# First group in six PSUM banks ordered by kind, early split of two mixed tiles, and another last statistic, in a one-layer streaming encoder

## The chip, the cores and the metric

One Trainium2 chip, one core. The metric is the device time of one launch in microseconds (us), the median of three runs. TensorE is PE (its weight loads PEld), VectorE DVE, ScalarE ACT, GpSimd POOL, and SyncE (SP) issues nearly all DMAs. PSUM has eight banks of 128 x 512 floats; the kernel gives six to products (`psm`) and two to small ones (`pst`).

## The reference, cut to what matters

2048 prompt positions and 8 x 16 sample positions (17 tiles of 128) go through one layer of three parallel mixers, then an output projection and a layer norm:

```python
h = jnp.einsum('btd,de->bte', x, w_in)                    # 1024 -> 2816
a, g_a, u, v, g_b, c1, c2, g_c = jnp.split(h, SPLITS, axis=-1)
y_a = pool_mixer(pool_ext, a, pos0, pool_w, pool_scale)   # trailing means 2/4/8/16, 64x64 products
v_n = layer_norm(v, gmlp_ln_g, gmlp_ln_b)
y_b = u * spatial_mix(v_n, gmlp_w, gmlp_b)                # lower-triangular 128x128 per head
c = c1 * jax.nn.sigmoid(c2)
y_c = conformer_tail(conv_ext, conv_w, ...)               # causal depthwise conv 31, LN, silu, 384x384
mixed = jnp.concatenate([silu(g_a) * y_a, silu(g_b) * y_b, silu(g_c) * y_c], axis=-1)
out = jnp.einsum('bte,ed->btd', mixed, w_out) + b_out     # 1024 -> 1024
x_new = layer_norm(ALPHA * x + out, ln_g, ln_b)
```

All values are float32. A large product is made of three: each operand is split into a rounded high part (`xhi`, `whi`, 32-bit values for the PE) and the rest (`xlo`, `wlo`), and high x high, high x low and low x high are added in PSUM.

## The kernel before

**Blocks and groups.** The 17 tiles are cut into blocks of 6, 6 and 5. For each block, eight groups of weight columns are multiplied one after another (`GROUPS`): group 0 is c2/0, c1/0, c2/1; group 1 is c1/1, c2/2, c1/2; then ga and a, v, gb, u, and group 7 is gc. x stands in eight rows k of 128 inputs (`XRow`; `xhi0` holds k=0 and 1, and so on), a group's weights in four pieces of two k each (`Piece`). `mm3` walks k from 0 to 7 and, at each k, over its outputs, with three matmuls for each: 12 matmuls a k where four outputs (banks) are open. In every block group 0 opens four banks for c2/0 and c1/0 (two halves of up to 384 columns each) and then walks all k again for c2/1.

**Splitting.** A load lands in one of four staging buffers (`stage`). ACT casts it to the high part, DVE subtracts to get the low part (`split`; the low part is recorded 1 us later by the planner's clock), and the subtraction frees the buffer for the next load. `Loader` keeps the four buffers full and splits a job when its `next` is called: by `hook(plan)` after the k of a group that the plan names, or by `after(us, fn)`. High and low weight parts go round in rings of six (`RING`). In block 0 each group's parts are also written to DRAM (`put`, tiles `keep`), and blocks 1 and 2 load them from there without splitting (`Kept`).

**Order.** Nothing is moved by a scheduler at run time: engines take their instructions in the order of the recording. `Clock.pe` counts planned PE time, `after` puts a function on a heap, and `poll` records what is due after each k. The 31 convolution taps of each channel tile (`conv`: `acc`, DVE, over all positions of the block) fill DVE whenever its planned clock is behind PE's; what is left at a block's end is recorded at once (`drain`), before the sums over channels (`csum`), whose low part `slo` the PE needs for `ps_mean`.

**Ends.** Mixed outputs go to DRAM tiles `mix`. During group 7 of block 2, `Mixed` loads whole tiles back (two staging buffers each) and `WPart` loads w_out in twelve parts (three for each pair of k, in the buffers of x that PE has left). The output projection opens four banks for tiles 0 and 1 together; two of them are banks that hold gc until ACT has taken its Silu (`sgc`). Then tiles 2 to 16 follow one by one. The last tile ends with its statistics (`lmv`), 1/sqrt(var + eps) as `inverse` on POOL (a multiply-add and a power), two passes on DVE in halves, and a store of each half.

The lines of the start that the change touches are these:

```python
    rows.append(XRow(0, k, lambda k=k: nc.sync.dma_start(out=w0[:, k, :], in_=wv[:, k, :])))
```

x rows 0 and 1 are loaded in two pieces each (384 columns), with one k of the first weights between the two pieces, and are split by halves.

Of the kernel before, what the change touches and what calls it, by code (L numbers as in the profile page):

```python
# [14 lines left out]
D = 1024  # L15
P = 128
# [57 lines left out]
def encoder_kernel(ctx: ExitStack, tc: tile.TileContext, a):  # L74
# [61 lines left out]

    warm = const.tile([P, 1], F32, name="warm")
    nc.vector.memset(warm, 0.0)
    nc.scalar.activation(out=warm, in_=warm, func=AF.Silu)
    mhalf = const.tile([P, 1], F32, name="mhalf")  # L140
    nc.gpsimd.memset(mhalf, -0.5)
    onec = const.tile([P, 1], F32, name="onec")
# [23 lines left out]
    class Piece:  # L166
# [7 lines left out]
        def split(self, then=None):  # L174
            hi = core.tile([P, 2, 384], F32R, tag="whi", bufs=RING, name="whi")
            lo = core.tile([P, 2, 384], F32R, tag="wlo", bufs=RING, name="wlo")
            split(hi[:, :self.n, :self.cols], lo[:, :self.n, :self.cols], self.st, then)
            ring.setdefault(self.key, []).append((hi, lo))
            if self.keep is not None:
                after(3, lambda: put(self.keep, hi, lo, self.cols))  # L180

    def put(keep, hi, lo, cols):
        for x, part in enumerate((hi, lo)):
# [15 lines left out]
        hi, lo = ring[key][k // 2]  # L199
        return hi[:, k % 2, c0:c0 + n], lo[:, k % 2, c0:c0 + n]  # L200

    def mm3(outs, kdim=KT, hook=None):

        for k in range(kdim):
            for ps, lhs, rhs in outs:
                lh, ll = lhs(k)
                rh, rl = rhs(k)
                nc.tensor.matmul(ps, lh, rh, start=(k == 0), stop=False)  # L208
                nc.tensor.matmul(ps, lh, rl, start=False, stop=False)  # L209
                nc.tensor.matmul(ps, ll, rh, start=False, stop=(k == kdim - 1))  # L210
# [11 lines left out]
    def w_in(key, g):  # L222

        w = len(GROUPS[g]) * P
        v = a["w_in"][:, gofs[g]:gofs[g] + KT * w].rearrange("p (k c) -> p k c", k=KT)
        if key[0] == 0:
            kept[g] = [dram.tile([P, 2, 2, w], F32, name=f"keep{g}_{k0}") for k0 in range(0, KT, 2)]
        keep = kept[g] if key[0] == 0 else [None] * (KT // 2)
        return [lambda k0=k0: Piece(key, v[:, k0:k0 + 2, :], w, keep[k0 // 2]) for k0 in range(0, KT, 2)]

    kept = {}
# [4 lines left out]
        w = len(GROUPS[g]) * P  # L236
        return [lambda k=k: Kept((b, g), k, kept[g][k], w, g % 2 == 1 and k < 2) for k in range(KT // 2)]

    def put_first():
        hi, lo = ring[0, 0][0]  # L240
        put(kept[0][0], hi, lo, 384)

    xhi = [None] * (KT // 2)
    xlo = [None] * (KT // 2)
# [40 lines left out]
    ring[0, 0] = [(whi0, wlo0)]  # L285
    rows = []
    for k in range(2):
        rows.append(XRow(0, k, lambda k=k: nc.sync.dma_start(out=w0[:, k, :], in_=wv[:, k, :])))
    w1 = wg[1]()
    for k in range(2):  # L290
        nc.vector.tensor_copy(whi0[:, k, :], w0[:, k, :])
        nc.vector.tensor_tensor(out=wlo0[:, k, :], in0=w0[:, k, :], in1=whi0[:, k, :].bitcast(F32),
                                op=ALU.subtract)
        rows[k].split(halves=True)
    w1.split()
    for k in range(2, KT, 2):
        rows = [XRow(0, k), XRow(0, k + 1)]
# [62 lines left out]
        nc.gpsimd.affine_select(out=w, in_=w, compare_op=ALU.is_ge, fill=0.0, base=0,  # L360
                                pattern=[[0, 4], [1, P]], channel_multiplier=-1)

    after(5, put_first)
    after(12, load_pool)
    after(24, load_v)
    after(130, load_small)
# [90 lines left out]
    def c_in(b, todo, wkey, hook=None):  # L457

        T, Tp = len(BLOCKS[b]) * P, prompt_width(b)
        runs, pss = [], {}  # L460
        for what, j, c0 in todo:
            if what == "c2":
                drain(j)
                ext = cp.tile([P, CONVC + TMAX], F32, tag=f"cext{j}", name=f"cext{j}")
                conv_state[(b, "ext", j)] = ext
                nc.gpsimd.tensor_copy(ext[:, 0:CONVC], halo_c[:, j, :])
            for t0, n in splits(T):
                ps = psm.tile([P, 512], F32, tag="mm", name="ps_c")
                pss[(what, j, t0)] = ps
                runs.append((ps[:, :n], lambda k, c0=c0: wslice(wkey, k, c0, P),  # L470
                             lambda k, t0=t0, n=n: xslice(k, t0, n)))
        if len(todo) > 1:
            mm3(runs)
        for what, j, c0 in todo:
            ext = conv_state[(b, "ext", j)]
            for t0, n in splits(T):
                if len(todo) == 1:
                    mm3([runs.pop(0)], hook=hook if t0 > 0 else None)
                ps = pss[(what, j, t0)]
                m = max(min(n, Tp - t0), 0)  # L480
                pieces = []
                if m > 0:
                    pieces.append((ext[:, CONVC + t0:CONVC + t0 + m], ps[:, :m]))
                if m < n:
                    pieces.append((exts[:, j, :, CONVC:], ps[:, m:n].rearrange("p (b t) -> p b t", b=NB)))
                for e, p in pieces:
                    if what == "c2":
                        nc.scalar.activation(out=e, in_=p, func=AF.Tanh, scale=0.5)
                    else:
                        vec.scalar_tensor_tensor(out=e, in0=e, scalar=1.0, in1=p,  # L490
                                                       op0=ALU.add, op1=ALU.mult)
            if what == "c1":
# [380 lines left out]
    def group_work(b, g, hook):  # L873
# [3 lines left out]
            {"v": b_v, "gb": b_gate, "u": b_u}[what](b, key, hook)  # L877
        elif what in ("c1", "c2"):
            todo = [(w, j, c * P) for c, (w, j) in enumerate(group)]
            if g == 0:  # L880
                c_in(b, todo[:2], key)
                todo = todo[2:]
            for i, t in enumerate(todo):
# [10 lines left out]
    for b in range(len(BLOCKS)):  # L894
# [4 lines left out]
        for g in range(LASTG):  # L899
            if b == 0 or (b, g + 1) == (LASTB, LASTG):  # L900
                loads = Loader([(fn, 1) for fn in w_in((b, g + 1), g + 1)])
                after(6, loads.next)
                after(9, loads.next)
                group_work(b, g, loads.hook({1: 1, 3: 1}))
            else:

                for i, fn in enumerate(w_kept(b, g + 1)):
                    after(10 + i if g % 2 == 0 and i < 2 else 5 + i, fn)
                group_work(b, g, None)
        if b == 0:  # L910
            W = w_kept(b + 1, 0)
            after(5, W[0])
            after(6, W[1])
            loads = Loader([(lambda k=k: XRow(b + 1, k), 1) for k in range(KT)])

            def leave(k):
                if k in (2, 4):
                    W[1 + k // 2]()
                if 2 <= k < 7:
                    loads.next()  # L920
# [54 lines left out]
    class WPart:  # L975
# [10 lines left out]
        def split(self, then=None):  # L986
# [9 lines left out]
                wo[kp] += [hi, lo]  # L996
            split(hi, lo, self.st[:, :n], then)

    jobs = [(lambda kp=kp, part=part: WPart(kp, part), 1) for kp in range(KT // 2) for part in range(3)]

    jobs[:0] = [(lambda q=q: Mixed(q), 2) for q in range(2)]
    jobs.insert(8, (lambda: Mixed(2), 2))
    loads = Loader(jobs)
    group_work(LASTB, LASTG, loads.hook({1: 2, 2: 1, 3: 2, 4: 1, 5: 2, 6: 1}))
    while loads.out:
        loads.next()
        flush()
# [35 lines left out]
    def out_finish(q, runs, together):  # L1043
# [19 lines left out]
        else:  # L1063

            mv = const.tile([P, 2], F32, name="lmv")
            vec.bn_aggr(out=mv, in_=last.rearrange("p a b -> p (a b)"))
            rs = inverse(mv, "l")
            halves = (slice(0, 512), slice(512, D))
            for c in halves:
                vec.scalar_tensor_tensor(out=y[:, c], in0=y[:, c], scalar=mv[:, 0:1], in1=bc["ln_g"][:, c],  # L1070
                                         op0=ALU.subtract, op1=ALU.mult)
# [107 lines left out]
```

## Time and profile before

| | |
|---|---|
| median of three runs | 776.77 us (776.49 to 778.35) |
| profiled execution | 778.33 us, span 776.6 us |
| PE busy | 765.1 us (99%), 4289 matmuls |
| DVE busy | 619.6 us (80%) |
| ACT busy | 195.5 us (25%) |
| POOL busy | 144.6 us (19%) |
| DMA | 132.91 MB, mean 171 GB/s |

Rows of a timeline read: start, duration (both us), engine, line, operation, out<-in, shape, count, and in brackets the idle time before it and what ended it. A matmul's duration overlaps the next one's; the step from start to start is what it costs. In rows of windows, (x...) counts instructions, and the last three numbers are granted PE clock, DMA share and GB/s. A row of waits reads: engine and instruction, what it waited for, total us, times, longest. A row of DMA issues ends with KB each and the median us from issue to landing. A row of a chain is start, length, engine, tile, line.

### The profile page before, as it was taken

The page shows a single profiled execution, that of the slowest core. Times are in us where ns is not written, and L with a number is a line of the kernel's source. Part 1 is how long each engine was busy: PE and PEld are TensorE (multiplying, and loading weights), DVE is VectorE, ACT ScalarE, POOL GpSimd, SP SyncE. Part 2 cuts the span into 40 slices and gives each one's busy share as a digit, 9 for nine tenths or more (in the row PEclk, how much of TensorE's full clock was granted, in tenths as well). Part 3 has the DMA queues.
Part 4 walks back from the last instruction along what each step waited for, and adds up shares of the span by engine and source line. Part 5 has one row for each costly group of instructions (what it writes and reads, how often), then busy time and mean ns, then how long its engine had stood idle before and what let it go on. Part 6 is the DMA issues. An engine that isn't in the chain of part 4 may idle for free.

```text
span 776.6 us, 11274 instructions
## 1 busy us (share of the span) xinstructions
PE 765.1 (99%) x4289; PEld 727.5 (94%) x4289; DVE 619.6 (80%) x916; ACT 195.5 (25%) x362; POOL 144.6 (19%) x172
## 2 busy tenths in 40 slices
PE   8999999999999999999999999999999999999996
PEld 6999999999999999999999999999988888888885
DVE  5799999999489989898147888899776987666665
ACT  5322314302412130220043122031261233232110
POOL 1010112300001011130002300151006244323241
PEclk9999999999999999999999999999999999999998
DMA  7975866359631465405655147363476434435411
GB/s 247 340 227 183 282 217 244 126 170 309 271 109 42 94 219 209 163 21 175 223 182 191 52 93 215 149 207 114 121 249 264 163 103 142 162 126 169 134 71 68
DMA packets 82118, 132.91 MB, mean 171 GB/s; under 512 B 25104, under 2 KB 48656, under 8 KB 82064
## 3 DMA queue, kind: packets, MB, share of 16 engines
q1 hardware_dynamic: 82064, 132.19, 51.5%
q8 instruction: 33, 0.54, 0.3%
q14 instruction: 21, 0.17, 0.1%
HBM read 90.52 MB, written 41.64 MB: 170 GB/s over the span
## 4 chain that ended last, share of the span: by engine, by line
PE 93%; DMA 3%; DVE 1%; SPq 1%; ACT 1%; issue 0%; POOLq 0%; DVEq 0%; POOL 0%; ACTq 0%
PE ps_o L208 8%; PE ps_o L209 8%; PE ps_o L210 8%; PE ps_c L208 6%; PE ps_c L209 6%; PE ps_c L210 6%; PE ps_gb L208 3%; PE ps_gb L209 3%; PE ps_gb L210 3%; PE ps_v L208 3%; PE ps_v L209 3%; PE ps_v L210 3%; PE ps_u L210 3%; PE ps_u L208 3%; PE ps_u L209 3%; PE ps_gc L210 2%
## 5 line engine op out<-in xcount | busy, mean ns | idle before, releaser
L131 DVE SCALAR_TENSOR_TENSOR acc<-cext,cw,acc 128x768 f32<-128x768 f32 (+1 forms) x270 | 257.7, 954 | 4.1
L208 PE MATMUL ps_o<-woxhi,mhi 128*128 128x512 f32 (+1 forms) x208 | 80.9, 389 | 1.2 <-ACT sgc L547 1.2
L209 PE MATMUL ps_o<-woxlo,mhi 128*128 128x512 f32 (+1 forms) x208 | 80.9, 389 | 0.0
L210 PE MATMUL ps_o<-woxhi,mlo 128*128 128x512 f32 (+1 forms) x208 | 80.3, 386 | 0.0
L208 PE MATMUL ps_c<-xhi,whi 128*128 128x384 f32 (+1 forms) x240 | 79.7, 332 | 0.4 <-ACT xhi L152 0.3
L209 PE MATMUL ps_c<-xlo,whi 128*128 128x384 f32 (+1 forms) x240 | 79.1, 330 | 0.8 <-DVE xlo L131 0.8
L210 PE MATMUL ps_c<-xhi,wlo 128*128 128x384 f32 (+1 forms) x240 | 78.6, 328 | 0.0
L208 PEld LDWEIGHTS ps_o<-woxhi,mhi 128*128 128x128 f32 x208 | 39.1, 188 | 9.8 <-ACT sgc L547 1.6
L209 PEld LDWEIGHTS ps_c<-xlo,whi 128*128 128x128 f32 x240 | 45.2, 188 | 2.2 <-DVE xlo L131 2.2
L208 PEld LDWEIGHTS ps_c<-xhi,whi 128*128 128x128 f32 x240 | 45.4, 189 | 1.5 <-ACT xhi L152 1.2
L210 PEld LDWEIGHTS ps_o<-woxhi,mlo 128*128 128x128 f32 x208 | 39.1, 188 | 8.2
L152 ACT CAST whi<-stage 128x768 fp32r<-128x768 f32 (+1 forms) x39 | 29.9, 770 | 66.2 <-PE ps_u L210 30.9
L131 DVE TENSOR_TENSOR xlo<-stage,xhi 128x768 fp32r<-128x768 f32 (+2 forms) x26 | 21.7, 853 | 31.0 <-ACT xhi L152 30.9
L209 PEld LDWEIGHTS ps_o<-woxlo,mhi 128*128 128x128 f32 x208 | 39.1, 188 | 7.5
L209 PE MATMUL ps_v<-wlo,xhi 128*128 128x384 f32 x136 | 45.5, 334 | 0.0
L208 PE MATMUL ps_v<-whi,xhi 128*128 128x384 f32 x136 | 45.5, 334 | 0.0
L210 PE MATMUL ps_v<-whi,xlo 128*128 128x384 f32 x136 | 45.5, 334 | 0.0
L208 PE MATMUL ps_u<-whi,xhi 128*128 128x384 f32 x136 | 45.4, 334 | 0.0
L209 PE MATMUL ps_u<-wlo,xhi 128*128 128x384 f32 x136 | 45.4, 334 | 0.0
L210 PE MATMUL ps_u<-whi,xlo 128*128 128x384 f32 x136 | 45.4, 334 | 0.0
L210 PEld LDWEIGHTS ps_c<-xhi,wlo 128*128 128x128 f32 x240 | 45.3, 189 | 0.0
L131 DVE TENSOR_TENSOR xr<-xr,ln_g 128x1024 f32<-128x1024 f32 x16 | 29.3, 1832 | 19.8 <-ACT xr L438 19.8
(210 smaller groups left out, 1916.9 us busy)
## 6 DMA issues: line engine op xcount, KB each, us to landing
whi<-keep SPq DMA_DIRECT2D x34, 384.0 KB, 6.0
wlo<-keep SPq DMA_DIRECT2D x34, 384.0 KB, 6.6
stage<-in_w_in SPq DMA_DIRECT2D x27, 384.0 KB, 4.7
keep<-whi SPq DMA_DIRECT2D x24, 384.0 KB, 4.3
keep<-wlo SPq DMA_DIRECT2D x24, 384.0 KB, 4.5
xr<-in_x_prompt SPq DMA_DIRECT2D x16, 512.0 KB, 5.0
o_y<-xr SPq DMA_DIRECT2D x16, 512.0 KB, 2.9
stage<-keep SPq DMA_DIRECT2D x20, 384.0 KB, 7.3
```

The lines of the kernel that those rows point to most:

```text
L131: return fn(*args, **kw)
L152: nc.scalar.copy(hi, src)
L208: nc.tensor.matmul(ps, lh, rh, start=(k == 0), stop=False)
L209: nc.tensor.matmul(ps, lh, rl, start=False, stop=False)
L210: nc.tensor.matmul(ps, ll, rh, start=False, stop=(k == kdim - 1))
```

## The change

1. In block 0, group 0 opens all six banks at once (c2/0, c1/0, c2/1). `mm3` has a parameter `early`: for k below 4 the matmuls of one k are ordered by kind (first half high x high for all outputs, then w high x x low, second half high x high, and so on) and not by output.
2. The first weights are loaded by ACT's queue, and the warm-up Silu stands behind these two issues. DVE makes their low part after the first half's low part of x.
3. Group 0 is no longer kept in block 0. In block 1 it is loaded from `w_in` and split again, through the staging buffers and mixed with the rows of x, and kept then (20 us after the split) for block 2. Group 0's loader splits group 1's pieces at k=3 and 5, not 1 and 3.
4. In the last group of block 2 the two first mixed tiles are split 4 and 5.5 us after its start by the planner's clock; the third comes last, behind all parts of w_out, and the plan of the hook is another.
5. For the last tile ACT makes var + eps (an Identity with a bias), POOL only the power; the parts are 640 and 384 columns.

```diff
-    nc.scalar.activation(out=warm, in_=warm, func=AF.Silu)
...
-                after(3, lambda: put(self.keep, hi, lo, self.cols))
+                after(3 if self.key[0] == 0 else 20, lambda: put(self.keep, hi, lo, self.cols))
...
-    def mm3(outs, kdim=KT, hook=None):
+    def mm3(outs, kdim=KT, hook=None, early=0):
         for k in range(kdim):
-            for ps, lhs, rhs in outs:
+            for half, kind in ((0, 0), (0, 1), (1, 0), (0, 2), (1, 1), (1, 2)) if k < early else ():
+                for ps, lhs, rhs in outs[half::2]:
+                    nc.tensor.matmul(ps, lhs(k)[kind == 2], rhs(k)[kind == 1],
+                                     start=(k == 0 and kind == 0), stop=False)
+            for ps, lhs, rhs in outs if k >= early else ():
...
-        if key[0] == 0:
+        keeps = key[0] == (1 if g == 0 else 0)
+        if keeps:
...
-        rows.append(XRow(0, k, lambda k=k: nc.sync.dma_start(out=w0[:, k, :], in_=wv[:, k, :])))
+        rows.append(XRow(0, k, lambda k=k: nc.scalar.dma_start(out=w0[:, k, :], in_=wv[:, k, :])))
+    nc.scalar.activation(out=warm, in_=warm, func=AF.Silu)
...
+    def first_low(k):
+        nc.vector.tensor_tensor(out=wlo0[:, k, :], in0=w0[:, k, :], in1=whi0[:, k, :].bitcast(F32),
+                                op=ALU.subtract)
     for k in range(2):
         nc.vector.tensor_copy(whi0[:, k, :], w0[:, k, :])
-        nc.vector.tensor_tensor(out=wlo0[:, k, :], in0=w0[:, k, :], in1=whi0[:, k, :].bitcast(F32),
-                                op=ALU.subtract)
-        rows[k].split(halves=True)
+        lows = [lambda k=k: first_low(k)]
+        rows[k].split(lambda: lows.pop()() if lows else None, halves=True)
...
-    after(5, put_first)
...
-            mm3(runs)
+            mm3(runs, hook=hook, early=4 if b == 0 else 0)
...
-            if g == 0:
+            if g == 0 and b == 0:
+                c_in(b, todo, key, hook)
+                todo = []
+            elif g == 0:
...
-                group_work(b, g, loads.hook({1: 1, 3: 1}))
+                group_work(b, g, loads.hook({1: 1, 3: 1} if (b, g) != (0, 0) else {3: 1, 5: 1}))
...
-            W = w_kept(b + 1, 0)
-            after(5, W[0])
-            after(6, W[1])
-            loads = Loader([(lambda k=k: XRow(b + 1, k), 1) for k in range(KT)])
...
-            group_work(b, LASTG, leave)
+            W = [(fn, 1) for fn in w_in((b + 1, 0), 0)]
+            X = [(lambda k=k: XRow(b + 1, k), 1) for k in range(KT)]
+            loads = Loader(W[:2] + X[:1] + W[2:3] + X[1:3] + W[3:] + X[3:])
+            group_work(b, LASTG, loads.hook({1: 1, 2: 1, 3: 2, 4: 2, 5: 2, 6: 2}))
             loads.next(3)
...
-    jobs[:0] = [(lambda q=q: Mixed(q), 2) for q in range(2)]
-    jobs.insert(8, (lambda: Mixed(2), 2))
-    loads = Loader(jobs)
-    group_work(LASTB, LASTG, loads.hook({1: 2, 2: 1, 3: 2, 4: 1, 5: 2, 6: 1}))
+    mix = [(lambda q=q: Mixed(q), 2) for q in range(3)]
+    loads = Loader(mix[:2] + jobs + mix[2:])
+    after(4, loads.next)
+    after(5.5, loads.next)
+    group_work(LASTB, LASTG, loads.hook({1: 1, 2: 2, 3: 1, 4: 2, 5: 1, 6: 2}))
...
-            rs = inverse(mv, "l")
-            halves = (slice(0, 512), slice(512, D))
+            rs = const.tile([P, 1], F32, tag="rs", bufs=4, name="lrs")
+            nc.scalar.activation(out=rs, in_=mv[:, 1:2], func=AF.Identity, scale=1.0, bias=eps)
+            nc.gpsimd.tensor_tensor(out=rs, in0=rs, in1=mhalf, op=ALU.pow)
+            halves = (slice(0, 640), slice(640, D))
```

Three places show what moves. A row is line, operation, out<-in with buffer numbers, and shape.

**PE, the first twelve products.** `ps_c_232` and `_233` are the two halves of c2/0 before (`_228` and `_229` after), `_234`, `_235` those of c1/0 (`_230`, `_231`); after, `_234` and `_235` are c2/1. Before:

```order
L208 MATMUL ps_c_232<-xhi0_110,whi_96 128x384
L209 MATMUL ps_c_232<-xlo0_111,whi_96 128x384
L210 MATMUL ps_c_232<-xhi0_110,wlo_97 128x384
L208 MATMUL ps_c_233<-xhi0_110,whi_96 128x384
L209 MATMUL ps_c_233<-xlo0_111,whi_96 128x384
L210 MATMUL ps_c_233<-xhi0_110,wlo_97 128x384
L208 MATMUL ps_c_234<-xhi0_110,whi_96 128x384
L209 MATMUL ps_c_234<-xlo0_111,whi_96 128x384
L210 MATMUL ps_c_234<-xhi0_110,wlo_97 128x384
L208 MATMUL ps_c_235<-xhi0_110,whi_96 128x384
L209 MATMUL ps_c_235<-xlo0_111,whi_96 128x384
L210 MATMUL ps_c_235<-xhi0_110,wlo_97 128x384
```

After:

```order
L207 MATMUL ps_c_228<-xhi0_105,whi_91 128x384
L207 MATMUL ps_c_230<-xhi0_105,whi_91 128x384
L207 MATMUL ps_c_234<-xhi0_105,whi_91 128x384
L207 MATMUL ps_c_228<-xlo0_106,whi_91 128x384
L207 MATMUL ps_c_230<-xlo0_106,whi_91 128x384
L207 MATMUL ps_c_234<-xlo0_106,whi_91 128x384
L207 MATMUL ps_c_229<-xhi0_105,whi_91 128x384
L207 MATMUL ps_c_231<-xhi0_105,whi_91 128x384
L207 MATMUL ps_c_235<-xhi0_105,whi_91 128x384
L207 MATMUL ps_c_228<-xhi0_105,wlo_92 128x384
L207 MATMUL ps_c_230<-xhi0_105,wlo_92 128x384
L207 MATMUL ps_c_234<-xhi0_105,wlo_92 128x384
```

Where the three products of one output stood together, three outputs now share one kind, and the low parts of w are wanted only by the tenth matmul.

**ACT from the last group of block 0 into block 1.** `sgc` is the Silu of gc, which frees its bank; `xhi` and `whi` are casts of the next block's rows and weights. Before:

```order
L547 ACTIVATE sgc_1847<-ps_gc_1849 128x384
L152 CAST xhi0_1969<-stage_1839 128x768
L152 CAST xhi0_1969<-stage_1841 128x768
L152 CAST xhi1_2009<-stage_1843 128x768
L152 CAST xhi1_2009<-stage_1845 128x768
L152 CAST xhi2_2043<-stage_1973 128x768
L547 ACTIVATE sgc_1847<-ps_gc_1921 128x384
L547 ACTIVATE sgc_1847<-ps_gc_1922 128x384
L547 ACTIVATE sgc_1847<-ps_gc_1923 128x384
L547 ACTIVATE sgc_1847<-ps_gc_1924 128x384
L152 CAST xhi2_2043<-stage_1990 128x768
```

After:

```order
L554 ACTIVATE sgc_1833<-ps_gc_1835 128x384
L151 CAST whi_1929<-stage_1825 128x768
L151 CAST whi_1948<-stage_1827 128x768
L151 CAST xhi0_1967<-stage_1829 128x768
L151 CAST whi_1970<-stage_1831 128x768
L151 CAST xhi0_1967<-stage_1933 128x768
L151 CAST xhi1_1992<-stage_1952 128x768
L151 CAST whi_2013<-stage_1974 128x768
L151 CAST xhi1_1992<-stage_1977 128x768
L151 CAST xhi2_2035<-stage_1996 128x768
L151 CAST xhi2_2035<-stage_1999 128x768
L554 ACTIVATE sgc_1833<-ps_gc_1899 128x384
```

Five casts stood between the second and the third Silu, now ten do, four of them weights.

**DVE at the same place**, from the last low parts of the next block's rows to the sums. `acc2` is a tap of the last channel tile, `csum` the sum over channels, `slo` its low part. Before:

```order
L131 TENSOR_TENSOR xlo1_2010<-stage_1845,xhi1_2009 128x768
L131 TENSOR_TENSOR xlo2_2044<-stage_1973,xhi2_2043 128x768
L131 TENSOR_TENSOR csum_2069<-acc0_363,acc1_518 128x384
L131 TENSOR_TENSOR csum_2069<-csum_2069,acc2_659 128x384
L131 TENSOR_TENSOR xlo2_2044<-stage_1990,xhi2_2043 128x768
L131 TENSOR_TENSOR xlo3_2065<-stage_2013,xhi3_2064 128x768
L131 TENSOR_TENSOR xlo3_2065<-stage_2029,xhi3_2064 128x768
L131 TENSOR_TENSOR slo_2073<-csum_2069,shi_2072 128x384
```

After:

```order
L131 TENSOR_TENSOR xlo1_1993<-stage_1977,xhi1_1992 128x768
L131 TENSOR_TENSOR xlo2_2036<-stage_1996,xhi2_2035 128x768
L131 TENSOR_TENSOR xlo2_2036<-stage_1999,xhi2_2035 128x768
L131 SCALAR_TENSOR_TENSOR acc2_641<-cext2_500,cw_173,acc2_641 128x768 x8
L131 TENSOR_TENSOR csum_2070<-acc0_416,acc1_499 128x384
L131 TENSOR_TENSOR csum_2070<-csum_2070,acc2_641 128x384
L131 TENSOR_TENSOR xlo3_2060<-stage_2018,xhi3_2059 128x768
L131 TENSOR_TENSOR xlo3_2060<-stage_2021,xhi3_2059 128x768
L131 TENSOR_TENSOR slo_2074<-csum_2070,shi_2073 128x384
```

Eight taps, which were done earlier before, now stand between the sixth row's low part and the sums.

**ACT ahead of the output projection.** `woxhi` and `whi` are parts of w_out, `mhi` the third mixed tile, `sgc` again the Silus that free banks. Before:

```order
L152 CAST woxhi1_5763<-stage_5710 128x768
L152 CAST woxhi1_5763<-stage_5728 128x768
L152 CAST whi_5786<-stage_5748 128x512
L152 CAST mhi_5808<-stage_5767 128x640
L152 CAST mhi_5808<-stage_5768 128x384
L547 ACTIVATE sgc_5596<-ps_gc_5660 128x384
L547 ACTIVATE sgc_5596<-ps_gc_5661 128x256
L547 ACTIVATE sgc_5596<-ps_gc_5662 128x384
```

After:

```order
L151 CAST woxhi1_5758<-stage_5700 128x768
L151 CAST woxhi1_5758<-stage_5719 128x768
L151 CAST whi_5779<-stage_5740 128x512
L151 CAST woxhi2_5800<-stage_5743 128x768
L151 CAST woxhi2_5800<-stage_5762 128x768
L151 CAST whi_5822<-stage_5783 128x512
L554 ACTIVATE sgc_5604<-ps_gc_5680 128x384
L554 ACTIVATE sgc_5604<-ps_gc_5681 128x256
```

Three more parts of w_out stand ahead of the Silus, and the third mixed tile is gone from there.

More of the change, by code (lines that the diff above doesn't have):

```diff
@@ L225, in w_in @@
         v = a["w_in"][:, gofs[g]:gofs[g] + KT * w].rearrange("p (k c) -> p k c", k=KT)
-        if key[0] == 0:
+        keeps = key[0] == (1 if g == 0 else 0)
+        if keeps:
             kept[g] = [dram.tile([P, 2, 2, w], F32, name=f"keep{g}_{k0}") for k0 in range(0, KT, 2)]
-        keep = kept[g] if key[0] == 0 else [None] * (KT // 2)
+        keep = kept[g] if keeps else [None] * (KT // 2)
         return [lambda k0=k0: Piece(key, v[:, k0:k0 + 2, :], w, keep[k0 // 2]) for k0 in range(0, KT, 2)]
@@ L237, in w_kept @@
         return [lambda k=k: Kept((b, g), k, kept[g][k], w, g % 2 == 1 and k < 2) for k in range(KT // 2)]
-    def put_first():
-        hi, lo = ring[0, 0][0]
-        put(kept[0][0], hi, lo, 384)
     xhi = [None] * (KT // 2)
@@ L910, in encoder_kernel @@
         if b == 0:
-            W = w_kept(b + 1, 0)
-            after(5, W[0])
-            after(6, W[1])
-            loads = Loader([(lambda k=k: XRow(b + 1, k), 1) for k in range(KT)])
[L916 to L920, printed above, removed]
-            group_work(b, LASTG, leave)
+            W = [(fn, 1) for fn in w_in((b + 1, 0), 0)]
+            X = [(lambda k=k: XRow(b + 1, k), 1) for k in range(KT)]
+            loads = Loader(W[:2] + X[:1] + W[2:3] + X[1:3] + W[3:] + X[3:])
+            group_work(b, LASTG, loads.hook({1: 1, 2: 1, 3: 2, 4: 2, 5: 2, 6: 2}))
             loads.next(3)
```

## The prediction

> **What bounds the kernel now.** I read the page first, then the waits of TensorE (PE), the busy time by windows, and the timelines of the three places where PE is not fed.
>
> ```profile
> PE 765.1 (99%) x4289; PEld 727.5 (94%) x4289; DVE 619.6 (80%) x916; ACT 195.5 (25%) x362; POOL 144.6 (19%) x172
> PE 93%; DMA 3%; DVE 1%; SPq 1%; ACT 1%; issue 0%; POOLq 0%; DVEq 0%; POOL 0%; ACTq 0%
> ...
> PE ps_o L208 <- ACT sgc L547: 1.2, 1, 1.2
> ...
> 0.00:25.00 25.00, 22.29 (x104) 18.14 (x105) 14.09 (x21) 13.69 (x20) 2.33 (x15) 1.00 0.79 247
> 75.00:100.00 25.00, 25.00 (x146) 25.00 (x145) 23.18 (x31) 8.63 (x15) 2.08 (x3) 1.00 0.85 282
> ```
>
> PE carries 93% of the chain. A full stretch of 25 us holds 146 matmuls; the first holds 104, eight of them warm-ups. The matmuls are the same in number and shape after the change, so the time moves only by what PE waits at the start, at hand-overs between blocks, and by what follows its last matmul. The 80% of VectorE (DVE) matter only where PE waits for one of its results.
>
> The profiled execution took 778.33 us, 1.7 of them outside its span of 776.6; the three runs have the median 776.77, 1.56 below it. I work out differences within the profiled execution and put them on the median. Under 0.3% (2.3 us: 774.4 to 779.1) a change of this kernel can't be told from none.
>
> **1. The first group in six banks, by kind.**
>
> ```profile
> 4.48 0.88 PE L208 MATMUL ps_c<-xhi,whi 128*128 128x384 f32 x1
> 5.24 0.69 PE L209 MATMUL ps_c<-xlo,whi 128*128 128x384 f32 x1
> 5.72 0.53 PE L210 MATMUL ps_c<-xhi,wlo 128*128 128x384 f32 x1
> 6.95 0.44 PE L209 MATMUL ps_c<-xlo,whi 128*128 128x384 f32 x1
> 7.40 0.34 PE L208 MATMUL ps_c<-xhi,whi 128*128 128x384 f32 x1
> 10.35 0.34 PE L210 MATMUL ps_c<-xhi,wlo 128*128 128x384 f32 x1
> 11.99 0.45 PE L209 MATMUL ps_c<-xlo,whi 128*128 128x384 f32 x1 [0.55 <-DVE xlo L131]
> 20.91 0.44 PE L209 MATMUL ps_c<-xlo,whi 128*128 128x384 f32 x1 [0.29 <-DVE xlo L131]
> ...
> 19.90 1.98 DVE L131 TENSOR_TENSOR xlo<-stage,xhi 128x768 fp32r<-128x768 f32 x2
> ```
>
> From 7.40 to 10.35 there are 17 steps of 0.173 us. The group has 144 matmuls. The one at 20.91 is number 74 (the second of k=6), and nothing waits behind it: the group ends at 20.91 + 71 x 0.173 = 33.2. Number 5 started at 6.95, so 140 matmuls (24.2 us) took 26.25: 2.05 us of waiting. With six banks each k is worth 18 matmuls, 3.1 us, where it was 12 and 2.1. Both halves of k=0 are there by 6.95, so from then on the six kinds run one after another; k=0 and k=1 last until about 12.1, k=7 is reached at about 28, and its last low part is there at 21.9 (19.90 + 1.98): no wait is left. Before 6.95 the only unwaited step is 0.48 (5.24 to 5.72); at that rate five matmuls start from 4.48, at twice 0.173 seven, instead of four. So the group ends between 6.95 + 137 x 0.173 = 30.7 and 31.0: **-2.4** (bounds -2.7 and -1.5, should the two queues that now load x and w together make the first x later). The warm-up Silu on ScalarE (ACT) stands behind two DMA issues of 0.4 now, and still ends near the first cast at 3.25.
>
> The evictions of this group stand on ACT behind all four casts of the next group's weights, and behind the cast of the pool weights:
>
> ```profile
> 22.28 0.42 SPq L184 DMA_DIRECT2D keep<-whi  x1
> 23.51 0.83 ACT L152 CAST whi<-stage 128x768 fp32r<-128x768 f32 x1 [1.15 <-DMA stage<-in_w_in]
> 31.97 3.19 SPq L349 DMA_DIRECT2D pw<-in_pool_w  x4
> 36.86 0.41 ACT L152 CAST poolwhi<-pw 128x256 fp32r<-128x256 f32 x1 [3.68 <-DMA pw<-in_pool_w]
> ```
>
> Before, SyncE's queue (SP) reached the four pool loads behind ten keep stores from 22.28; now behind four, of which the last needs the low part that follows the cast at 23.51: 23.51 + 0.83 and 0.95 to 1.0 of DVE, 25.3. The loads are out 3.2 later (28.5) and land, as before (36.86 against 35.16), 1.7 later: 30.2. Cast 0.41, first tanh 0.49: a bank is free at 31.1, and PE wants one at 30.8. **+0.4** (0 to +1.5). The eight keep stores of this group come back on SP in block 1, 20 us after its splits; there PE is fed from parts that are long in SBUF, so I count nothing for them.
>
> **2. Block 0 to block 1.** This group's weights now come through the staging buffers, cast and subtracted again: four ACT casts (0.84 each) and four DVE subtractions (0.95). ACT's four Silus that free PE's banks stand behind ten casts, not five, and six of the ten DMAs wait for a buffer that DVE frees.
>
> ```profile
> 175.81 11.52 DVE L131 SCALAR_TENSOR_TENSOR acc<-cext,cw,acc 128x768 f32<-128x768 f32 x11
> 195.78 0.84 ACT L152 CAST xhi<-stage 128x768 fp32r<-128x768 f32 x1 [5.48 <-DMA stage<-in_xT]
> 196.52 1.63 ACT L547 ACTIVATE sgc<-ps_gc 128x384 f32<-128x384 f32 x4
> 196.85 0.33 PE L208 MATMUL ps_c<-xhi,whi 128*128 128x384 f32 x1
> 202.37 0.55 DVE L131 TENSOR_TENSOR slo<-csum,shi 128x384 fp32r<-128x384 f32 x1
> 209.49 0.34 PE ps_mean L571 x2
> ...
> stage<-in_w_out SPq DMA_DIRECT2D x8, 256.0 KB, 3.7
> stage<-in_w_out SPq DMA_DIRECT2D x4, 384.0 KB, 3.6
> stage<-in_w_out SPq DMA_DIRECT2D x4, 128.0 KB, 3.0
> ```
>
> In the clock of these rows: nine taps of 1.045 from 175.81 (eleven before) end at 185.2, then DVE alternates low parts and taps: W0 to 186.1, W1 to 188.1, row 0 to 190.0, W2 to 190.9. Each end lets one load go. Loads of 384 KB from w_out land after 3.6 (the last three rows; 3.0 for the small ones is the lower end). Row 2's load goes at 188.1, is cast by 192.5 and subtracted by 193.5; row 5's load goes then and is cast by 197.9. The first Silu (0.49) ends at 198.4, and PE wants that bank six matmuls after 196.85, at 197.9: **+0.5**. Two landings lie in this chain, so the wait is 0 from 3.3 down and 1.3 at 4.0, my estimate for six loads that compete. Then DVE: low part of row 5 (0.95), eight taps that were done earlier before (8.4), the two sums (1.15), rows 6 and 7 (1.95), and only then the low part that the ps_mean matmul wants (0.55): 13.0 us after row 5's cast, 210.9, where it stood at 202.9. PE reaches ps_mean at 209.4 plus the wait just counted, 209.9: **+1.0** (0 to +1.4).
>
> **3. Into the output projection.**
>
> ```profile
> 555.63 1.85 SPq L957 DMA_DIRECT2D stage<-mix  x4
> ...
> 558.54 0.73 ACT L152 CAST mhi<-stage 128x640 fp32r<-128x640 f32 x1 [2.06 <-DMA stage<-mix]
> 570.13 0.62 ACT L152 CAST whi<-stage 128x512 fp32r<-128x512 f32 x1 [0.61 <-DMA stage<-in_w_out]
> ...
> 569.74 0.95 DVE L131 TENSOR_TENSOR woxlo<-stage,woxhi 128x768 fp32r<-128x768 f32 x1
> ...
> 571.22 0.39 PE L210 MATMUL ps_o<-woxhi,mlo 128*128 128x512 f32 x1
> 572.81 0.50 PE L208 MATMUL ps_o<-woxhi,mhi 128*128 128x512 f32 x1 [1.21 <-ACT sgc L547]
> ...
> 573.55 0.23 PE ps_o L210
> ```
>
> PE could go on one step of 0.23 after 571.22, at 571.45, and does at 572.81: it waits 1.36 for a Silu that stands on ACT behind the third mixed tile. The early split of two mixed tiles is cheap to price: their cast at 558.54 waited for a load that SP issued at 555.63, behind twelve stores of turned tiles, and these stand ahead of it still. So they are cast at the same time as before, and with them every w_out part up to the sixth (570.13). But now nine parts stand ahead of the Silu, not six and the mixed tile. The ninth needs the buffer of the fifth, free when DVE ends at 570.69, lands 3.0 to 3.7 later, is cast in 0.62, and the Silu takes 0.49: 574.8 to 575.5. PE waits 3.4 to 4.1 in place of 1.36: **+2.2** (+2.0 to +2.7). The third mixed tile, now last, is needed only about 20 us later.
>
> **4. The last tile.**
>
> ```profile
> 770.41 0.68 POOL L427 TENSOR_SCALAR lrs<-lmv 128x1 f32<-128x1 f32 x1 [8.97 <-DVE lmv L131]
> 771.17 0.94 POOL L428 TENSOR_TENSOR lrs<-lrs,mhalf 128x1 f32<-128x1 f32 x1
> 772.15 1.41 DVE L131 SCALAR_TENSOR_TENSOR xr<-xr,lrs,ln_b 128x512 f32<-128x512 f32 x2 [0.44 <-POOL lrs L428]
> ...
> L598 ACT ACTIVATE cvar<-ps_var,eps x6: 262/263/264, 219.6 to 640.4; 128x3 f32<-128x3 f32 x5, 128x2 f32<-128x2 f32 x1
> ```
>
> An ACT operation like L598 (0.26) replaces 0.68 on GpSimd (POOL): -0.42, and DVE, idle 0.44 there, can use 0.4. The unequal parts sum to the same DVE time; the last store shrinks from 256 to 192 KB, for which I take -0.05. **-0.45** (-0.7 to 0, should the extra crossing between engines eat it).
>
> **Sum:** -2.4 + 0.4 + 0.5 + 1.0 + 2.2 - 0.45 = +1.25, on the median 776.77: **778.0**.
>
> **Rivals.**
>
> *The early split is early.* If the mixed loads left SP about 3 us sooner, every cast to the ninth part would move with them, and the Silu would be done near 571.5: step 3 gives -1.4, the sum -2.35, the time 774.4. For it: ACT sits idle for 2.06 ahead of 558.54. Against it: the same stores stand ahead of the loads on SP. Chance 0.17.
>
> *No delay between the blocks.* If row 5's load lands by 195.5, step 2 gives nothing, the sum is -0.25: 776.5. For it: fewer loads compete there. Against: the eight taps stand ahead of the sums in DVE's order. Chance 0.12.
>
> *PE's clock falls in the long wait, and it ends slower.*
>
> ```profile
> 771.00:772.00 1.00, 0.00 (x0) 0.00 (x0) 0.70 (x2) 0.00 (x0) 0.92 (x2) 0.69 0.00 0
> ...
> 768.79 0.28 PE L210 MATMUL ps_o<-whi,mlo 128*128 128x256 f32 x1
> ```
>
> From 771 to 772 the granted clock is 0.69 on average: halved at about 771.4, 2.3 us after PE's last matmul ended (768.79 + 0.28). The wait of step 3 was 1.36 and becomes 3.4 or more. Where the fall hits, the matmuls behind it run at half rate: at the start full rate came only at 6.95, 5.5 us after the first warm-up, which bounds the loss at 2.75; I take 2.0, so 780.0. It decides from a wait of about 2.3 us, and against it stands that the moment of the fall need not come inside the wait. Chance 0.27, with the upper bounds of the other terms that end there too. The Trainium skill ("TensorE: Matmul & The Clock Gate", Part 1 and the closing table) says the same of gaps over about 3 us: a window of some 3.4 us, free-running, found idle halves the clock, and a busy one restores it. By that rule an estimate of the loss is half of 3.4, or 1.7, and the time 779.7; the trace's fall after 2.3 us shows that a partly idle window can do.
>
> **How the numbers follow.** My sum has 0.44; it, the second rival and a third of the first lie within 0.3% of 776.77 (0.44 + 0.12 + 0.05, rounded to 0.60), two thirds of the first is faster (0.12, and 0.01 for all lower bounds together), the third rival is slower (0.27). The range of 774.3 to 780.6 takes in the first and third rival and leaves out the lower and upper bounds met together.
>
> **What would show it.** Step 1: the first group's matmuls continuous from 7 us and ending near 31; a wait of its successor for a tanh on ACT. Step 2: PE waiting for Silu L554 near 195 and, 12 us later, ps_mean for slo on DVE. Step 3: PE's wait for Silu L554 over 3 us near 570, the mixed casts still just behind their loads; a clock digit below 9 right after it would be the third rival. Step 4: the last DVE pass under 0.1 us after its statistic. I am wrong if SP reaches the mixed loads sooner, or if the loads between the blocks land well under 3 us.

## The result, and the profile after

| | before | after |
|---|---|---|
| median of 22 executions | 776.86 us (776.25 to 778.35) | 782.01 us (777.12 to 784.80) |
| ratio, 95% interval | | 1.0054 [1.0044, 1.0064] |
| profiled execution | 778.33, span 776.6 | 780.75, span 779.0 |

The change makes the kernel 0.54% slower by the ratio, which is close to that of the means; the medians are 5.15 us (0.66%) apart. Its executions spread over 7.7 us where those of before spread over 2.1. The profiled execution of the changed kernel is a mild one, 1.3 us under its median; that of before, with 778.33, lies at the slow end of its 22.

The page's busy line, the windows (the last three columns are granted PE clock, DMA share, GB/s) and the waits of PE, after:

```profile
PE 764.9 (98%) x4289; PEld 728.2 (93%) x4289; DVE 623.7 (80%) x920; ACT 198.3 (25%) x367; POOL 139.6 (18%) x171
```

```profile
0.00:25.00 25.00, 23.41 (x124) 21.16 (x125) 13.92 (x21) 13.41 (x19) 2.47 (x16) 1.00 0.78 243
...
575.00:600.00 25.00, 25.00 (x106) 20.35 (x105) 15.03 (x28) 4.59 (x8) 9.34 (x7) 0.95 0.68 249
```

```profile
PE ps_c L212 <- ACT cext L495: 2.9, 1, 2.9
PE ps_o L212 <- ACT sgc L554: 2.4, 1, 2.4
```

The first 25 us hold 124 matmuls in place of 104: the new start works. Two waits of PE on ACT then eat it, one of 2.9 us behind the first group and one of 2.4 ahead of the output projection. And a stretch behind the second shows a granted clock of 0.95, which the kernel before does not have.

**The start and its hand-over.** Timeline of the profiled execution before, PE:

```profile
33.18 0.33 PE L210 MATMUL ps_c<-xhi,wlo 128*128 128x384 f32 x1
33.35 0.33 PE L208 MATMUL ps_c<-xhi,whi 128*128 128x384 f32 x1
```

After, PE, then ACT, then SP:

```profile
4.87 0.76 PE L207 MATMUL ps_c<-xhi,whi 128*128 128x384 f32 x3
5.47 0.70 PE L207 MATMUL ps_c<-xlo,whi 128*128 128x384 f32 x3
...
29.77 0.34 PE L214 MATMUL ps_c<-xhi,wlo 128*128 128x384 f32 x1
33.00 0.45 PE L212 MATMUL ps_c<-xhi,whi 128*128 128x384 f32 x1 [2.90 <-ACT cext L495]
...
32.15 0.40 ACT L151 CAST poolwhi<-pw 128x256 fp32r<-128x256 f32 x1 [3.63 <-DMA pw<-in_pool_w]
32.47 1.25 ACT L495 ACTIVATE cext<-ps_c 128x384 f32<-128x384 f32 x3
...
17.06 6.45 SPq L171 DMA_DIRECT2D stage<-in_w_in  x4
25.33 1.19 SPq L183 DMA_DIRECT2D keep<-wlo  x1
26.62 3.22 SPq L357 DMA_DIRECT2D pw<-in_pool_w  x4
```

The group's last matmul starts at 29.77, before at 33.18: 3.4 us gained. The next matmul starts at 33.00, before at 33.35, so 0.35 is left. In between PE waits for a tanh, which stands on ACT behind the cast of the pool weights, which waits for loads that SP has out only at 29.84.

**Into the output projection.** PE, ACT, and then windows cut at the moments where the clock record changes:

```profile
571.27 0.39 PE L214 MATMUL ps_o<-woxhi,mlo 128*128 128x512 f32 x1
574.01 0.57 PE L212 MATMUL ps_o<-woxhi,mhi 128*128 128x512 f32 x1 [2.35 <-ACT sgc L554]
...
572.95 0.62 ACT L151 CAST whi<-stage 128x512 fp32r<-128x512 f32 x1
573.48 1.41 ACT L554 ACTIVATE sgc<-ps_gc 128x384 f32<-128x384 f32 x4
```

```profile
570.88:574.30 3.42, 1.07 (x5) 0.60 (x4) 2.89 (x5) 3.01 (x6) 0.00 (x0) 1.00 0.76 229
574.30:577.71 3.41, 3.41 (x9) 2.64 (x9) 3.41 (x7) 2.24 (x4) 0.00 (x0) 0.50 0.82 247
577.71:581.12 3.41, 3.41 (x16) 2.77 (x15) 2.61 (x4) 1.52 (x3) 0.00 (x0) 1.00 0.58 201
```

The Silu stands behind the ninth w_out part, as foreseen; PE waits 2.5 us: it could have gone on a step of 0.23 after 571.27, at 571.50. Then follow 3.41 us at clock 0.50: nine matmuls where the window after holds sixteen.

**The last tile.** PE, ACT, POOL, DVE:

```profile
771.49 0.28 PE L214 MATMUL ps_o<-whi,mlo 128*128 128x256 f32 x1
772.73 0.24 DVE L131 BATCH_NORM_AGGREGATE lmv<-last 128x2 f32<-128x18 f32 x1
...
773.06 0.29 ACT L1073 ACTIVATE lrs<-lmv,eps 128x1 f32<-128x1 f32 x1 [7.64 <-DVE lmv L131]
773.43 0.86 POOL L1074 TENSOR_TENSOR lrs<-lrs,mhalf 128x1 f32<-128x1 f32 x1 [9.29 <-ACT lrs L1073]
774.33 1.41 DVE L131 SCALAR_TENSOR_TENSOR xr<-xr,lrs,ln_b 128x640 f32<-128x640 f32 x2
```

From the last matmul's start to the end of the span it is 7.54 us, before 7.84: 0.3 gained.

### The profile page after: what moved, and what is told of

It is laid out like the page before. It is cut to its first block, busy times and chain, and to the rows that moved or that the text cites. A ratio compares the mean times of both kernels' runs of the same rounds, so it can differ in the third digit from the quotient of the medians.

```text
span 779.0 us, 11275 instructions
## 1 busy us (share of the span) xinstructions
PE 764.9 (98%) x4289; PEld 728.2 (93%) x4289; DVE 623.7 (80%) x920; ACT 198.3 (25%) x367; POOL 139.6 (18%) x171
## 4 chain that ended last, share of the span: by engine, by line
PE 90%; DMA 4%; DVE 2%; issue 2%; ACT 1%; SPq 1%; POOL 0%; POOLq 0%; DVEq 0%; ACTq 0%
PE ps_o L212 8%; PE ps_o L213 8%; PE ps_o L214 8%; PE ps_c L212 5%; PE ps_c L214 5%; PE ps_c L213 5%; PE ps_gb L212 3%; PE ps_gb L213 3%; PE ps_gb L214 3%; PE ps_v L214 3%; PE ps_v L213 3%; PE ps_v L212 3%; PE ps_u L212 3%; PE ps_u L214 3%; PE ps_u L213 3%; PE ps_gc L212 2%
## 5 line engine op out<-in xcount | busy, mean ns | idle before, releaser
L212 PE MATMUL ps_c<-xhi,whi 128*128 128x384 f32 (+1 forms) x216 | 70.8, 328 | 2.9 <-ACT cext L495 2.9
L214 PE MATMUL ps_c<-xhi,wlo 128*128 128x384 f32 (+1 forms) x216 | 70.4, 326 | 0.0
L213 PE MATMUL ps_c<-xlo,whi 128*128 128x384 f32 (+1 forms) x216 | 70.4, 326 | 0.0
L151 ACT CAST whi<-stage 128x768 fp32r<-128x768 f32 (+1 forms) x43 | 33.3, 776 | 62.4 <-DMA mix<-yt 15.7
L445 ACT ACTIVATE xr<-xr,onm,ors 128x1024 f32<-128x1024 f32 x16 | 19.9, 1246 | 101.9 <-POOL onm L441 101.9
L131 DVE SCALAR_TENSOR_TENSOR xr<-xr,ps_o 128x512 f32<-128x512 f32 (+1 forms) x35 | 23.1, 668 | 28.4 <-PE ps_o L214 27.4
L131 DVE TENSOR_TENSOR wlo<-stage,whi 128x768 fp32r<-128x768 f32 (+1 forms) x43 | 38.7, 906 | 7.4 <-ACT whi L151 5.0
```

The source lines that it names most:

```text
L131: return fn(*args, **kw)
L151: nc.scalar.copy(hi, src)
L445: nc.scalar.activation(out=out, in_=src, func=AF.Identity, scale=rs, bias=nm_)
```

## The experiments

Theory: the time goes into the two waits, and each of them can besides halve the clock for a while behind it, which makes the median worse than the profiled execution. Rival: the waits cost their length alone, and the rest lies elsewhere. Ratios are to the kernel before, on the same chip.

### Without the first wait

```diff
-    after(12, load_pool)
-    after(24, load_v)
+    after(20, load_pool)
+    after(32, load_v)
```

> The changed kernel with the pool weights loaded and cast later, so that no cast of theirs stands on ACT ahead of the four tanhs that free the first group's banks. Theory: PE's wait of 3.05 us at 30 us goes, and with it a fall of the granted clock that costs 1.7 us in most runs: median 777.3 to 778 (from 782.0), mean clock from 0.994 to about 0.996. Rival (the first wait costs only itself; what the median has beyond the profiled execution comes from elsewhere, such as loads that land later in other executions): 779.0, clock still 0.994.

Measured: 777.59 (775.5 to 779.86), ratio 1.0012 [1.0002, 1.0022]. The pool cast now stands behind the four tanhs and PE runs through at 30 us. Against the changed kernel that is 4.4 us less by the medians and 3.3 by the ratios (1.0054 against 1.0012), more than the 1.7 us that the wait measures on average in the eight profiled executions below. `load_v` moves with the pool loads; what that does by itself no run shows. The mean clock is 0.995 to 0.998 where the changed kernel has 0.991 to 0.994 in 14 of 22 executions. This bears the theory out; the rival had 779.0, over the interval's 778.4.

### Without the second wait

```diff
-    mix = [(lambda q=q: Mixed(q), 2) for q in range(3)]
-    loads = Loader(mix[:2] + jobs + mix[2:])
-    after(4, loads.next)
-    after(5.5, loads.next)
-    group_work(LASTB, LASTG, loads.hook({1: 1, 2: 2, 3: 1, 4: 2, 5: 1, 6: 2}))
+    jobs[:0] = [(lambda q=q: Mixed(q), 2) for q in range(2)]
+    jobs.insert(8, (lambda: Mixed(2), 2))
+    loads = Loader(jobs)
+    group_work(LASTB, LASTG, loads.hook({1: 2, 2: 1, 3: 2, 4: 1, 5: 2, 6: 1}))
```

> The changed kernel with the order of before in the last group of block 2 (the third mixed tile behind six parts of w_out). Theory: PE's wait ahead of the output projection goes back from 2.5 to 1.36 us (-1.2) and is too short for a fall of the clock (-1.7 in the runs that had one): median 779.0 to 779.5, mean clock about 0.996. Rival: 780.8, the clock as low as in the changed kernel.

Measured: 776.37 (775.08 to 777.24), ratio 0.9993 [0.9984, 1.0001], clock 0.996 to 0.999. This is 2.6 us lower than the lower end of what I expected, and further from the rival: the old order's wait is mostly not 1.36. In four profiled executions with that order PE waited 1.36 (before), 0.60 (last tile alone, below), 0.42 (this one) and 0.33 (both edits), against 2.3 to 2.8 in all eight of the changed kernel.

### Without either

Both edits.

> Both edits together. Theory: no wait over 1.5 us is left, so no fall of the clock: the start's 3.2 us and the last tile's 0.3 us show in full, median 773.2 to 774.5, all runs within 1.5 us, mean clock 0.997 or more. Rival: -3.0 and -1.2 from 782.0, 777.8, with the wide spread of the changed kernel.

Measured: 774.32 (773.73 to 774.61), ratio 0.9969 [0.9957, 0.998]. The waits of PE in it, and the matmul that waited:

```profile
PE wps L280 <- POOL wz L277: 1.5, 1, 1.5
PE ps_o L212 <- ACT sgc L554: 0.2, 1, 0.2
```

```profile
569.17 0.51 PE L212 MATMUL ps_o<-woxhi,mhi 128*128 128x512 f32 x1 [0.17 <-ACT sgc L554]
```

All of the 7.7 us (6.6 by the ratios) by which the changed kernel is worse than this one come from the places of these two orders, and the rest of the change is a gain of 2.4 us.

### The last tile alone

On the kernel before, part 5 of the change.

> The kernel before with the edit of the last tile alone (var + eps by ACT, parts of 640 and 384). Theory: -0.3 us as the changed kernel's last tile shows (0.53 less to the last DVE pass, 0.19 more behind it): 776.5. Rival (prediction): -0.45, 776.4; rival: no change, 776.9.

Measured: 776.55 (775.81 to 777.07), ratio 0.9998 [0.9989, 1.0006]: a gain too small to tell. Its profile shows the mechanism all the same: from the statistic to the last DVE pass 1.60 us (769.08 to 770.68), before 2.13 (770.02 to 772.15).

### A control

> The changed kernel unaltered, as a control beside the others on one chip. The two undone parts gave 777.6 and 776.4 and both together 774.3, which adds up to 779.6 for the changed kernel where it measured 782.0. Theory (the two waits act on each other, through the clock): 781.5 to 782.5 again, with a wide spread and a clock of 0.993 to 0.994 in most runs. Rival (the parts add up and the first measurement met another chip or hour): 779.6, clock about 0.996.

Measured: 781.39 (779.95 to 782.12), ratio 1.0052 [1.004, 1.0064]. The slowdown is the kernel's and not the hour's. By the medians the parts do not add up: 774.3 with 3.3 for the second wait and 2.05 for the first gives 779.6. By the ratios they come to 1.0036 against 1.0052 here, a difference no wider than the intervals, so that the two waits act on each other is not shown.

### The order of the last group alone, on the kernel before

The diff of the second experiment, turned round.

> The kernel before with the changed order of the last group of block 2 alone. Theory: the longer wait ahead of the output projection and one fall of the clock in most runs, +2.8 to +3.5: 779.5 to 780.2, clock about 0.996. Prediction's step 3 without a fall: +2.2, 778.9, clock unchanged. Rival (it is worth what its undoing gave in the changed kernel, 5.6): 782.3.

Measured: 780.55 (778.77 to 784.23), ratio 1.0053 [1.0036, 1.007]. The median lies a little over the theory's 779.5 to 780.2. The interval shuts out the prediction's step without a fall (778.9) and reaches the rival's 782.3 with its upper end alone. The profiled execution was the slowest, 784.23. In its windows PE waits 3.2 us across an edge at 574.26, and the half rate lasts two windows:

```profile
570.85:574.26 3.41, 1.22 (x6) 0.67 (x4) 2.43 (x5) 1.71 (x3) 0.00 (x0) 1.00 0.78 249
574.26:577.68 3.42, 2.40 (x6) 1.92 (x7) 3.42 (x7) 3.29 (x7) 0.00 (x0) 0.50 0.79 270
577.68:581.09 3.41, 3.41 (x10) 2.64 (x9) 2.41 (x4) 1.82 (x4) 0.00 (x0) 0.50 0.65 200
```

### A longer wait, made to order

On the kernel with both edits, four and ten Silus more ahead of the one that PE waits for:

```diff
+                for _ in range(4 if b == LASTB and j == 1 and t0 == 0 else 0):
+                    nc.scalar.activation(out=sg[:, j, t0:t0 + n], in_=r[0], func=AF.Silu)
                 nc.scalar.activation(out=sg[:, j, t0:t0 + n], in_=r[0], func=AF.Silu)
```

> The kernel with both edits (774.3) where ACT computes the Silu of the first bank of the last gc matmuls five times and not once, with the same output: 4 x 0.35 us more of wait for PE ahead of the output projection, about 1.9 to 2.3 in all. Theory (a fall needs a wait of about 2.3 us or more): +1.4 and a fall in a minority of the runs, median 775.7 to 776.2. Rival (any wait over 1.4 can bring the fall): 777.4 with the clock down by 0.002.

> The same with eleven Silus: 10 x 0.35 us more of wait, about 4 to 4.4 in all. Theory: +3.5 for the wait and 1.7 for one fall in every run: 779.5, clock lower by 0.002 than without. Rival (the fall comes early in such a wait and is over before PE works again): 777.8, clock lower by 0.002 all the same. Rival (two windows at half rate): 781.2.

Measured: 778.43 (777.19 to 780.48), ratio 1.0018 [1.0009, 1.0027], and 781.71 (781.33 to 782.88), ratio 1.0063 [1.0051, 1.0075]. I had the Silu too cheap: one more takes 0.52 us from start to start and not 0.35, so PE waits 2.7 us with four more and 5.9 with ten. With four, a wait of 2.7, 2.35 more than without, costs 4.1 (3.8 by the ratios); the clock is 0.996 in nine executions of ten and the profiled one has a fall, worth 1.6. The wait came out over my bound of 2.3 as well as over the rival's 1.4, so this run does not choose between the two; that 2.3 is too high is shown by the falls behind waits of 1.97 and 2.23 us near 30 in the table below. With ten more, 5.5 us of wait cost 7.4. The measured 781.7 is near the 781.2 of the rival with two windows by luck, the wait being 1.5 us longer than the longest I had planned. Its windows show why it is not two falls' worth:

```profile
567.89:571.31 3.42, 0.75 (x4) 0.28 (x2) 3.19 (x7) 3.26 (x8) 0.00 (x0) 1.00 0.83 261
571.31:574.72 3.41, 0.37 (x1) 0.37 (x2) 0.14 (x1) 3.25 (x8) 0.00 (x0) 0.50 0.36 138
574.72:578.14 3.42, 3.42 (x9) 2.65 (x9) 2.16 (x3) 3.21 (x6) 0.00 (x0) 0.50 0.04 9
578.14:581.55 3.41, 3.41 (x16) 2.79 (x16) 1.31 (x3) 0.83 (x1) 0.00 (x0) 1.00 0.93 250
```

Two windows are at half rate, but PE sleeps through nearly all of the first.

### Six more profiled executions of the changed kernel

Open was what the executions at the median have that the profiled one had not.

> The changed kernel unaltered, one profiled execution more, to see where the clock falls in an execution near its median of 782. The two executions profiled so far took 780.75 and 779.95, with one fall of 3.41 us at the output projection in each. Theory: in an execution of 781.5 or more the half rate at the projection lasts two windows, 6.83 us, as it did in the one of 784.2 with the last group's order alone, and none falls near 30 us. Rival: two separate falls, one behind the first group's wait at 30 to 33 us and one at the projection.

> The same again, one profiled execution: an execution of 781.5 or more shows 6.83 us at half rate at the projection (theory) or two falls of 3.41 at the two waits (rival); one of 779 to 781 shows one fall of 3.41; one under 778.5 none.

> The same again, one profiled execution: an execution of 781.5 or more shows 6.83 us at half rate at the projection (theory) or two falls of 3.41 at the two waits (rival); one of 779 to 781 shows one fall of 3.41; one under 778.5 none.

> The changed kernel unaltered, one profiled execution. Of the five so far, four of 779.6 to 780.8 had one fall of 3.41 us at the projection and the one of 782.1 had a second one behind the first group's wait. Theory (the two waits each bring falls): an execution over 781.5 has two falls of 3.41, one at 31 to 37 us and one at the projection. Rival: 6.83 us at the projection alone.

> The same, one profiled execution more: over 781.5 two falls of 3.41, one at 31 to 37 us and one at the projection (theory) or 6.83 us at the projection alone (rival); 779 to 781 one fall.

> The same, one profiled execution more: over 781.5 two falls of 3.41, one at 31 to 37 us and one at the projection (theory) or 6.83 us at the projection alone (rival); 779 to 781 one fall.

The waits are start-to-start steps less the full-rate step (0.17 and 0.23); the first row is the profiled execution of the result.

| execution | us | wait near 30 | wait near 571 | falls of the clock at |
|---|---|---|---|---|
| result | 780.75 | 3.06 | 2.51 | 574.3 |
| control | 779.95 | 0.97 | 2.82 | 573.2 |
| further a | 780.01 | 1.79 | 2.49 | 573.1 |
| further b | 782.09 | 2.23 | 2.29 | 33.6 and 576.3 |
| further c | 779.59 | 1.24 | 2.34 | 573.6 |
| further d | 779.36 | 1.59 | 2.42 | 572.5 |
| further e | 781.32 | 1.97 | 2.45 | 33.0 and 575.8 |
| further f | 780.61 | 0.81 | 2.47 | 574.0 |

Each fall here lasts 3.41 us. The two executions over 781 have two falls at two waits, and all others one. Ahead of the first three I had expected a double window at the projection and put the two separate falls down as the rival: the rival holds, and ahead of the last three I had turned to it. The windows of further b around both waits:

```profile
30.21:33.62 3.41, 1.35 (x8) 1.03 (x7) 0.94 (x2) 1.76 (x5) 0.00 (x0) 1.00 0.78 291
33.62:37.03 3.41, 3.41 (x13) 3.41 (x12) 3.30 (x6) 0.23 (x2) 0.27 (x1) 0.50 1.04 322
...
572.92:576.34 3.42, 1.29 (x6) 0.85 (x5) 3.31 (x6) 2.97 (x8) 0.00 (x0) 1.00 0.76 249
576.34:579.75 3.41, 3.41 (x9) 2.65 (x9) 3.41 (x7) 1.46 (x2) 0.00 (x0) 0.50 0.58 198
```

### A version that beats both

Both edits, and the third mixed tile behind the Silus of the last banks:

```diff
-    group_work(LASTB, LASTG, loads.hook({1: 2, 2: 1, 3: 2, 4: 1, 5: 2, 6: 1}))
+    group_work(LASTB, LASTG, loads.hook({1: 2, 2: 1, 3: 2, 4: 1, 5: 2}))
```

> Both edits, and the third mixed tile split behind the Silus of the last gc banks and not ahead of them (the plan of the last group's hook without its last entry). What is left of PE's wait ahead of the output projection (0.33 us in the profiled execution of the kernel with both edits, 1.36 in that of the kernel before) goes: 773.3 to 774.1. Rival (the w_out parts, now 1.3 us later on ACT, are missed two k further on): 774.3 or more, a wait of PE for a woxhi part some 6 us into the projection.

Measured: 773.82 (772.83 to 774.29), ratio 0.9955 [0.9942, 0.9969]. No wait of PE at the projection is left; the two that remain:

```profile
PE wps L280 <- POOL wz L277: 1.5, 1, 1.5
PE ps_mean L578 <- DVE slo L131: 0.2, 1, 0.2
```

It is 3 us faster than the kernel before. Against the version with both edits (0.9969) the intervals overlap, so the last step alone is not shown.

## Why the prediction was wrong, step by step

**The start (-2.4): right, a little small.** Over the eight executions of the table the group's last matmul starts at 29.77 to 30.83, mean 30.35, where it was 33.18: -2.8.

**The pool cast (+0.4, bound 1.5): the first term that failed.** The wait was 0.8 to 3.1 us, mean 1.7. I had the chain of SP, load, cast and tanh right and each link too short: the fourth keep store left SP at 26.5 and not 25.3, the loads were all issued at 29.84 and not 28.5, and landed 2.3 us later and not 1.7; PE came 0.9 earlier besides. Above all I priced the wait by its length alone. Undoing it alone gave 4.4 us by the medians and 3.3 by the ratios.

**Between the blocks (+0.5 and +1.0): too large.** From matmul 1000 to matmul 1300 in PE's order (the stretch with both waits) it is 51.49 us in all three profiled executions with the old order of the blocks and 51.54 to 52.44 in fourteen with the new, mean 51.91: +0.4. The expected wait for a bank was not there, only that of ps_mean:

```profile
PEld ps_mean L578 <- DVE slo L131: 0.3, 1, 0.3
```

**Into the projection (+2.2): the size of the wait right by luck, its consequence left out.** The wait is 2.3 to 2.8, not the 3.4 to 4.1 I worked out: the mixed loads left SP at 553.57 and not 555.63, so the early split was 2 us early, 2 of the 3 us that my first rival asked for:

```profile
553.57 3.33 SPq L961 DMA_DIRECT2D stage<-mix  x4
```

But I compared with the 1.36 of one execution, at the slow end of its 22, and in the other three with the old order the wait is 0.33 to 0.60. So the difference is about 2, as forecast. What the sum left out is the fall of the clock, my third rival (chance 0.27, price 2.0): it came in all eight profiled executions and cost 1.6, from 27.1 to 28.7 us for the 118 matmuls behind the wait. I had also taken the least wait that brings it for 2.3 us, from the one fall behind the last matmul; what counts is the idle share of one window of the clock, as the last section shows.

**The last tile (-0.45): right, a little large.** It is 0.3 in the profiled execution: the last pass starts 0.53 sooner behind the statistic, and what follows it takes 0.2 longer, where I had taken the smaller store for 0.05 shorter. The run of this part alone is too noisy to confirm it.

The sum with measured terms, on 776.8: -2.8 + 0.4 - 0.3 gives 774.1 (774.3 measured without the waits). With 1.7 and 2.1 for the waits (2.47 less the 0.33 of the version with both edits), 1.6 for the fall at the projection and a quarter of 1.7 for the other it is 779.9; the eight executions of the table have a mean of 780.5. The forecast of 778.0 fails by taking the first wait for 0.4 and the clock for a rival at one place only. The median of 782.0 needs one fall more than these eight mostly have. Its executions have that by their mean clock, of which one fall takes 0.002 (half of 3.41 us in 780) and which does not tell where the fall was: 14 of 22 are at 781.6 or more with a clock of at most 0.994, the clock that the two profiled ones with two falls have (0.994; the others 0.995 to 0.996). Three more of the 22, 777.1 to 778.4, are at 0.998 or 0.999; the profiled executions without a fall ahead of the last tile have 0.997 or 0.998, so these three had none either. Why the second fall comes in 14 of 22 there and in 2 of these 8 stays open; the six further ones ran on another chip than the control, and no run tells whether that matters. So does why it did not come, by the clock (0.996 to 0.999, as in the kernel before), in the eleven executions of the kernel that has the first wait alone.

## What to carry to other kernels

A wait of PE costs more than its length once it takes up over half of one 3.4 us window of the clock (between 1.6 and 1.8 us here): add 1.6 to it, and expect executions to spread. When a stage is made faster, follow every queue up to the instruction that frees its banks: here ACT held a cast of something needed much later ahead of the evictions, and moving it by 8 us of plan, together with the old order at the projection, gave the gain back.

## What the runs showed of the hardware

**The clock is decided on a fixed grid.** In the 17 profiled executions of this study every change of the clock record in the middle lies on a grid of 3.413 us that starts where the record first has full rate, at 4.2 to 7.4 us, another place each time. How long PE is busy in one window sets the rate of the next. Around 30 us, one fence each: further e, further a, the kernel with the first wait alone, and the result:

```profile
29.62:33.03 3.41, 1.61 (x10) 1.29 (x9) 0.85 (x2) 1.68 (x5) 0.00 (x0) 1.00 0.84 319
33.03:36.45 3.42, 3.42 (x12) 3.42 (x11) 3.31 (x6) 0.62 (x2) 0.26 (x1) 0.50 0.98 313
```

```profile
30.38:33.79 3.41, 1.79 (x11) 1.47 (x10) 1.40 (x4) 1.94 (x5) 0.24 (x1) 1.00 0.83 319
33.79:37.20 3.41, 3.41 (x21) 3.41 (x20) 3.30 (x4) 0.46 (x1) 0.03 (x1) 1.00 1.01 325
```

```profile
30.27:33.68 3.41, 1.92 (x11) 1.60 (x10) 1.53 (x4) 1.94 (x5) 0.27 (x1) 1.00 0.93 360
33.68:37.09 3.41, 3.41 (x21) 3.41 (x21) 3.30 (x4) 0.62 (x1) 0.00 (x0) 1.00 1.00 315
```

```profile
28.16:31.58 3.42, 1.94 (x12) 1.62 (x10) 0.96 (x1) 0.36 (x1) 0.00 (x0) 1.00 0.81 307
31.58:34.99 3.41, 1.99 (x11) 1.99 (x12) 1.97 (x5) 1.94 (x5) 0.26 (x1) 1.00 1.03 383
```

PE busy for 1.61 of 3.41 us: half rate in the next window. Busy for 1.79, 1.92, 1.94: full rate. The edge lies between, about half of the window. Over the 17 executions every window at full rate with at most 1.61 busy us is followed by half rate, and every one with 1.79 or more by full rate. The result's wait is the longest of these four, 2.9 us, and brings no fall, because an edge at 31.58 cuts it into 1.48 and 1.42. At half rate 2.40 busy us were not enough to come back (the order alone, above), while 3.03 were in further a (573.09 to 576.51).

The Trainium skill ("TensorE: Matmul & The Clock Gate", Part 1) has a free-running window of 3413 ns, with which these records agree. Its closing table sets the limit at idle gaps over about 3 us; here 1.8 us in one window were enough, and 2.9 across two were not.

**One wait of one kernel came out at 0.8 to 3.1 us.** In the eight executions of the table the first group's last matmul starts within 1.1 us (29.77 to 30.83) and the one behind the tanh within 1.3 (31.70 to 33.00), and the result's execution has the earliest of the one and the latest of the other.
